# Loading the memory into a tile of x, turning it among the last sums, and reordering the loads and scalings around a pooling mixer

## The chip, the cores and the metric

The program runs on one core of a Trainium2 chip, in one launch. The metric is the device time of one execution in microseconds (us); lower is better. Before the change three runs took 1949.14, 1951.25 and 1950.2 us, so the median is 1950.2 us.

## What is computed

The reference is a decoder trunk over 512 tokens of width 1024, batch 1, depth 2. Each of the two layers is: half a SwiGLU feed-forward network (FFN), a token mixer, cross-attention into 256 memory tokens, a second half FFN. Each of the four ends in `X = LayerNorm(alpha * X + sublayer)`. Layer 0's mixer is a differential attention, layer 1's a causal pooling mixer. The two parts that the change touches are, cut to what matters:

```
def pool_mixer(x, w_grp, b_grp, scale):        # 4 groups of 256 columns, windows 2, 4, 8, 16
    pooled = (mean of the last w tokens) - x    # for each group g its own window w
    y = einsum('bsgc,gcd->bsgd', pooled, w_grp) + b_grp
    return y.reshape(B, S, D) * scale

def memory_cross_attention(x, mem, wq, wkv, wo):
    q = x @ wq                                  # 4 heads of 256
    k, v = split(mem @ wkv, 2)                  # 256 memory tokens
    o = softmax(q k^T / 16) v, head by head
    return o @ wo
```

All inputs are float32.

## The kernel before

**Numbers.** TensorE works in float32r, a rounded form of float32. Every operand is therefore split in two, `split` (L116): ScalarE (ACT) casts it to the high part (L119, names that end in `h`), VectorE (DVE) subtracts that from the source to get the low part (L120, names in `l`). A product is three matmuls, high by high, high by low, low by high (`mm3`, L198, shown as L202, L203, L204). A weight block of 1024 by 256 (1 MB) arrives as one `raw` tile and is split in two halves of 128x1024, that is two casts and two subtractions.

**X and its factors.** X lives as four token tiles of 128x1024. For matmuls it is split, where needed after a turn (a TensorE transpose), into factors that lie in the two `xh` and two `xl` tiles, which each phase claims anew (`new_xt`, L453).

**The place of the change** is layer 1, between the end of its first FFN and its cross-attention. The FFN's last products are sums into tokens, `plain_down` (L858), in the order of the table `LAST`, eight of them, each 18 matmuls of 128x512 (`ps<-ha,xe`, `ps<-hb,xe`). After a token's second sum its LayerNorm runs (`ln_token`, L361, with the long DVE operations at L379 and L381).

Then `mixer` (L1520) runs two things beside each other. `early_kv` (L1395) computes keys and values of the first two heads from the memory alone: `xa_kv` (L1323) loads the head's key weights (`raw_cols`, L230, `raw<-in_xa_wkv_dram`), makes 48 matmuls `pk`, loads the value weights, makes 48 matmuls `pv`, and does so for the second head. `pool_mixer` (L1237) makes the band products that pool over the windows (`pp`, eight chunks), splits each into `pooled`, multiplies by the pool's weights `pw`, adds to X (L357) and runs the LayerNorm token by token; after each LayerNorm the token is turned (L482) into factors for the cross-attention. `weave` (L207) interleaves the two on TensorE by a count of estimated time: a first step of the mixer after 4300 ns of key and value work, then one for every 900 ns. The cross-attention's queries (`xq`) follow.

Ahead of all this `load_memory` (L1297) loads `mem` into a tile of the `raw` pool and turns it, 16 transposes in four groups of four, each group into a PSUM bank of `aux`, and splits the result into `mem0h` to `mem6l`. `pool_weights` (L1202) loads the pool's weights (1 MB), and for each half of the columns a row of scales and a row of biases, each broadcast to 256 KB; it multiplies the weights by the scales (`pw<-pw,ps`, L1232) and prepares the bias.

**What sets the order.** All of these loads are issued by SyncE (SP) in one queue, in the order of the program, and SP waits at each load until its tile is free. `raw` has two buffers, so a load of weights waits until the splits of the load two before it are done. The rows of gain and bias for the LayerNorm (`load_row`, L325, issued at L334 as `pooled<-in_ln_g_dram` and `pooled<-in_ln_b_dram`) are in the same queue and take tiles of the tag `pooled`. Within an engine the instructions stand in an order that a scheduler fixes when the program is built, from priorities and dependencies; `issue_after` keeps an instruction behind a given one. Pools of SBUF follow each other in the order in which they are opened (`stage_pools`, L168), and a tile of a new pool waits until whatever of the old phase lay there is done.

Of the kernel before, what the change touches and what calls it, by code (L numbers as in the profile page):

```python
# [9 lines left out]
F32 = mybir.dt.float32  # L10
# [3 lines left out]
ALU = mybir.AluOpType  # L14
# [3 lines left out]
P = 128  # L18
D = 1024
S = 512  # L20
# [89 lines left out]
class Trunk:  # L110
# [56 lines left out]
    @contextmanager  # L167
    def stage_pools(self, w, raw, order):  # L168

        with ExitStack() as ctx:  # L170
            self.stage = {}
            for n in order:
                if n == "wl" and order[0] == "mem" or n == "wh" == order[0]:
                    self.to_w(ctx)
                self.stage[n] = ctx.enter_context(self.pool(n))
            self.banks = {n: ctx.enter_context(self.pool(n, space=PSUM)) for n in ("px", "py", "yz")}
            self.w_bufs, self.raw_bufs, self.aux_turn = w, raw, 0
            yield
# [679 lines left out]
    def plain_down(self, w, layer, j, ln, beside):  # L858
# [35 lines left out]
        for n, (half, t) in enumerate(LAST):  # L894
            if n == 2:
                if (layer, j) == (1, 0):
                    self.pool_bands()
                self.begin_ln(layer, ln, 2.0)
                for k in (1, 2):
                    operand(0, k)  # L900
                for tok in range(2):
                    for k in (1, 2):
                        product(sums[tok], 0, tok, k)
                    self.summed(0, tok, 1.0, sums[tok])
            ps = self.aux("ps", ("yz", "py")[n % 2])
            if n < 2:
                sums.append(ps)
                product(ps, half, t, 0)
                yield
                continue  # L910
            for k in range(3):
                if t == 0:
                    operand(half, k)
            if self.last_ln and t == NT - 1:
                parts = [(ps, slice(0, S))]
                if half:
                    parts = [(ps[:, : 2 * P], slice(0, 2 * P))]
# [281 lines left out]
            self.bandl, braw[:, :, 1, :16], self.bandf[:, :, :16].bitcast(F32)  # L1199
        )  # L1200

    def pool_weights(self):  # L1202

        nc = self.nc
        w = self.a["pool_w"][0].rearrange("g k n -> (g k) n")
        self.pool_w = self.tmp("pw", (P, KC, 256))
        nc.sync.dma_start(self.pool_w, w.rearrange("(k p) n -> p k n", p=P))
        rows = self.a["pool_b"].rearrange("l g c -> l (g c)")

        bias = self.pair("pb")  # L1210
        for half in range(2):
            c = slice(half * S, (half + 1) * S)
            sc, bs = self.tmp("ps"), self.tmp("ps")
            nc.sync.dma_start(sc, self.a["pool_scale"][:, c].to_broadcast([P, S]))
            nc.sync.dma_start(bs, rows[:, c].to_broadcast([P, S]))
            nc.vector.tensor_tensor(bs, bs, sc, ALU.mult)
            nc.vector.tensor_scalar(
                bias[half].rearrange("p (a n) -> p a n", n=P),
                self.ident[:, None].to_broadcast([P, NT, P]),
                0.0,  # L1220
                None,
                ALU.mult,
            )
            nc.scalar.copy(bias[half][:1], bs[:1])
            nc.scalar.copy(bias[half][32:33], bs[32:33])
            nc.vector.tensor_sub(
                bias[half][32:33], bs[32:33], bias[half][32:33].bitcast(F32)
            )
            for g in range(2):
                r = self.pool_w[:, 4 * half + 2 * g : 4 * half + 2 * g + 2]  # L1230
                f = sc[:, None, g * 256 : (g + 1) * 256].to_broadcast([P, 2, 256])
                nc.vector.tensor_tensor(r, r, f, ALU.mult)  # L1232
# [64 lines left out]
    def load_memory(self, tag=None):  # L1297
# [6 lines left out]
                for h in range(2):  # L1304
                    nc.sync.dma_start(raw[m][h], src[:, m, h])
        else:
            t = self.raw_tile((2, 2, S))
            nc.sync.dma_start(t, src)
            raw = [[t[:, m, h] for h in range(2)] for m in range(2)]
        self.memT = []  # L1310
        for c in range(0, KC, 2):
            pt = self.aux("pt").rearrange("p (c m n) -> p c m n", c=2, m=2)
            for i in range(2):
                for m in range(2):
                    o = (c + i) % 4 * P
                    self.nc.tensor.transpose(pt[:, i, m], raw[m][c // 4][:, o : o + P], self.ident)
            t = tuple(self.stage["mem"].tile([P, 2, MEM], F32R, name=f"mem{c}{n}") for n in "hl")
            self.split(t[0], t[1], pt.rearrange("p c m n -> p c (m n)"))
            self.memT += [(t[0][:, i], t[1][:, i]) for i in range(2)]
        if tag and LINE < 480:  # L1320
            self.stage["mem"].tile([P, (480 - LINE) // 4], F32, name="mempad")

    def xa_kv(self, w, h):  # L1323
        nc = self.nc
        rk = self.raw_cols(w, h * 256)
        ps = self.mm("pk").rearrange("p (c n) -> p c n", c=2)
        for j in range(2):
            wk = self.cols(rk, j)
# [7 lines left out]
        kt = kv()  # L1336
        self.turn_late()
        self.split(kt[0], kt[1], ps)
        wv = self.wide(self.raw_cols(w, D + h * 256))
        ps = self.mm("pv").rearrange("p (m n) -> p m n", m=2)  # L1340
        for m in range(2):
            o = slice(m * P, (m + 1) * P)
# [49 lines left out]
            self.oT.append(o)  # L1392
            yield

    def early_kv(self, layer, heads):  # L1395
        for h in range(heads):
            self.kv.append((yield from self.xa_kv(self.a["xa_wkv"][layer], h)))

    def xa_main(self, layer):
        wq, wkv = self.a["xa_wq"][layer], self.a["xa_wkv"][layer]  # L1400
# [119 lines left out]
    def mixer(self, layer, ln):  # L1520
# [65 lines left out]
```

## Time and profile before

| | before |
|---|---|
| median of three runs (lowest, highest) | 1950.2 us (1949.14, 1951.25) |
| span of the profiled execution | 1944.6 us |
| median less that span | 5.6 us |
| TensorE (PE) busy | 98% of the span |
| VectorE (DVE), ScalarE (ACT), GpSimd (POOL) busy | 81%, 53%, 15% |

The page shows one profiled execution; its own time is not listed apart from its span, and the median of the runs stands 5.6 us above the span. Views say which engine is busy (PE matmuls, PEld weight loads beside them), in which stretch, at which granted TensorE clock (PEclk, 1.00 is full speed), and what ended each wait ("idle before <- releaser"). Times of rows are us from the start of the span. A row's busy time of a matmul includes its way through the pipeline, so 171 matmuls of 278 ns fit in 20 us; their pitch, the number in a full stretch, is what one more costs.

### The profile page before, as it was taken

The page shows a single profiled execution, that of the slowest core. Times are in us where ns is not written, and L with a number is a line of the kernel's source. Part 1 is how long each engine was busy: PE and PEld are TensorE (multiplying, and loading weights), DVE is VectorE, ACT ScalarE, POOL GpSimd, SP SyncE. Part 2 cuts the span into 40 slices and gives each one's busy share as a digit, 9 for nine tenths or more (in the row PEclk, how much of TensorE's full clock was granted, in tenths as well). Part 3 has the DMA queues.
Part 4 walks back from the last instruction along what each step waited for, and adds up shares of the span by engine and source line. Part 5 has one row for each costly group of instructions (what it writes and reads, how often), then busy time and mean ns, then how long its engine had stood idle before and what let it go on. Part 6 is the DMA issues. An engine that isn't in the chain of part 4 may idle for free.

```text
span 1944.6 us, 32554 instructions
## 1 busy us (share of the span) xinstructions
PE 1913.0 (98%) x13122; PEld 1748.4 (90%) x13122; DVE 1566.7 (81%) x2215; ACT 1025.8 (53%) x1582; POOL 300.0 (15%) x266
## 2 busy tenths in 40 slices
PE   8999999999999999999999999999999999999998
PEld 8999998888778888999998999999888889999997
DVE  7888889888867557888888988898787458988886
ACT  6555554566655434655554655555455336555553
POOL 2112121111210001211220311212000003111210
PEclk9999999999999999999999999999989999999999
DMA  9978772322134316977785687877254338877861
GB/s 239 218 163 185 167 144 77 90 68 85 44 119 141 109 66 184 185 174 162 143 193 174 109 180 163 183 168 153 78 173 131 104 107 155 176 163 171 183 132 60
DMA packets 247031, 277.96 MB, mean 143 GB/s; under 512 B 8288, under 2 KB 212576, under 8 KB 246880
## 3 DMA queue, kind: packets, MB, share of 16 engines
q0 software_dynamic: 92928, 92.29, 31.1%
q1 hardware_dynamic: 153952, 183.59, 29.4%
q8 instruction: 103, 1.69, 0.4%
q14 instruction: 48, 0.39, 0.1%
HBM read 273.75 MB, written 2.10 MB: 142 GB/s over the span
## 4 chain that ended last, share of the span: by engine, by line
PE 82%; DVE 10%; issue 4%; ACT 2%; DMA 1%; POOL 1%; SPq 0%; DVEq 0%; POOLq 0%; ACTq 0%
PE x L202 7%; PE x L203 7%; PE x L204 7%; PE z L203 4%; PE z L202 4%; PE z L204 4%; PE ps L202 3%; PE ps L204 3%; PE ps L203 3%; PE px L202 2%; PE px L204 2%; PE px L203 2%; PE x L674 2%; DVE wl L120 2%; PE y L204 2%
## 5 line engine op out<-in xcount | busy, mean ns | idle before, releaser
L659 POOL DMA_DIRECT2D ra<-in_ffn_w_in_dram x132 | 170.2, 1303 | 1002.8 <-DVE wl L120 701.2
L119 ACT CAST wh<-ra 128x1024 fp32r<-128x1024 f32 x184 | 193.7, 1053 | 225.3 <-PE x L203 70.5
L120 DVE TENSOR_TENSOR wl<-ra,wh 128x1024 fp32r<-128x1024 f32 x184 | 224.6, 1224 | 72.0 <-ACT wh L119 71.2
L119 ACT CAST wh<-rc 128x1024 fp32r<-128x1024 f32 x136 | 143.2, 1053 | 121.6 <-PE x L203 41.9
L202 PE MATMUL x<-xe,wh 128*128 128x256 f32 x704 | 195.4, 278 | 0.0
L203 PE MATMUL x<-xe,wh 128*128 128x256 f32 x704 | 195.2, 277 | 0.0
L204 PE MATMUL x<-xe,wl 128*128 128x256 f32 x704 | 195.1, 277 | 0.0
L120 DVE TENSOR_TENSOR wl<-rc,wh 128x1024 fp32r<-128x1024 f32 x136 | 165.1, 1223 | 29.1 <-ACT wh L119 28.8
L119 ACT CAST wh<-b 128x1024 fp32r<-128x1024 f32 x112 | 117.8, 1052 | 134.2 <-PE x L203 68.7
L120 DVE TENSOR_TENSOR wl<-b,wh 128x1024 fp32r<-128x1024 f32 x112 | 137.1, 1224 | 41.3 <-ACT wh L119 41.3
L202 PE MATMUL x<-xh,wh 128*128 128x256 f32 x544 | 151.3, 278 | 0.0
L203 PE MATMUL x<-xl,wh 128*128 128x256 f32 x544 | 150.9, 277 | 0.0
L204 PE MATMUL x<-xh,wl 128*128 128x256 f32 x544 | 150.9, 277 | 0.0
L203 PEld LDWEIGHTS x<-xe,wh 128*128 128x128 f32 x704 | 132.5, 188 | 1.3
L202 PEld LDWEIGHTS x<-xe,wh 128*128 128x128 f32 x704 | 132.1, 188 | 1.3
L204 PEld LDWEIGHTS x<-xe,wl 128*128 128x128 f32 x704 | 132.5, 188 | 0.0
L120 DVE TENSOR_TENSOR wl<-raw,wh 128x1024 fp32r<-128x1024 f32 x64 | 80.6, 1265 | 54.5 <-ACT wh L119 53.8
L203 PEld LDWEIGHTS x<-xl,wh 128*128 128x128 f32 x544 | 102.5, 188 | 0.7
L202 PEld LDWEIGHTS x<-xh,wh 128*128 128x128 f32 x544 | 102.1, 188 | 0.7
L119 ACT CAST wh<-raw 128x1024 fp32r<-128x1024 f32 x64 | 66.7, 1050 | 68.1 <-PE xq L203 22.6
L204 PEld LDWEIGHTS x<-xh,wl 128*128 128x128 f32 x544 | 102.4, 188 | 0.0
L204 PE MATMUL y<-xh,wl 128*128 128x256 f32 x352 | 98.4, 280 | 1.0 <-DVE wl L120 0.2
(436 smaller groups left out, 6331.4 us busy)
## 6 DMA issues: line engine op xcount, KB each, us to landing
ra<-in_ffn_w_in_dram POOLq DMA_DIRECT2D x132, 512.0 KB, 6.8
rc<-in_ffn_w_in_dram SPq DMA_DIRECT2D x88, 512.0 KB, 5.8
b<-in_ffn_w_out_dram SPq DMA_DIRECT2D x76, 512.0 KB, 4.7
ra<-in_ffn_w_in_dram SPq DMA_DIRECT2D x44, 512.0 KB, 5.3
rc<-in_ffn_w_in_dram POOLq DMA_DIRECT2D x44, 512.0 KB, 7.0
raw<-in_xa_wkv_dram SPq DMA_DIRECT2D x16, 1024.0 KB, 5.5
raw<-in_da_w_qkv_dram SPq DMA_DIRECT2D x16, 512.0 KB, 5.1
raw<-in_xa_wq_dram SPq DMA_DIRECT2D x8, 1024.0 KB, 5.1
```

The lines of the kernel that those rows point to most:

```text
L119: self.nc.scalar.copy(hi, src),
L120: self.nc.vector.tensor_sub(lo, src, hi.bitcast(F32)),
L202: mm(out, w[0], x[0], start=start, stop=False, skip_group_check=again)
L203: mm(out, w[0], x[1], start=False, stop=False, skip_group_check=again)
L204: self.last_mm = mm(out, w[1], x[0], start=False, stop=stop, skip_group_check=again)
L659: nc.gpsimd.dma_start(t, source(*block), accum_op=ALU.add)
L674: self.last_mm = nc.tensor.matmul(ps[:, j], v[i][:, k, j * P : (j + 1) * P], x[l][:, k], start=n == i == l == 0, stop=n == 7 and i == 1, s ...
```

## The change

Five things are changed, all of them in layer 1 between the FFN and the cross-attention.

1. The memory is loaded into a tile of `xtp` with the tag `xh` (named `memraw`), not into a tile of `raw`. All its 16 turns are placed behind one matmul, `amid`, the last of the third of the eight sums of `plain_down` (n == 2 there); their four PSUM tiles come from `mm`, `px` and `aux`.
2. The key and the value weights of head 0 are both requested ahead of the mixer and handed to `xa_kv` as `raws`.
3. `pool_weights` is cut in two. `pool_loads` requests the weights and all four rows at once (`ps` has four buffers now), `pool_weights` does the scaling, and is called after the pooled chunk 1, behind that chunk's split on DVE. The zeros and ones that DVE wrote (three `tensor_scalar`) are three memsets on POOL.
4. The pools are opened in the order `wh`, `wl`, `mem`, `raw`, with the pads of `to_w` and `to_x` ahead of `wh` and `mem`.
5. The numbers of `weave` are 640 and 8500 for 900 and 4300.

```diff
-                if n == "wl" and order[0] == "mem" or n == "wh" == order[0]:
+                if n == "wh" == order[0]:
                     self.to_w(ctx)
+                if n == "mem":
+                    self.to_x(ctx)
...
             self.summed(half, t, 1.0, ps)
+            if n == 2:
+                self.amid = self.last_mm
             few(beside, 6)
...
-    def pool_weights(self):
+    def pool_loads(self):
...
         nc.sync.dma_start(self.pool_w, w.rearrange("(k p) n -> p k n", p=P))
-        rows = self.a["pool_b"].rearrange("l g c -> l (g c)")
-
-        bias = self.pair("pb")
+        self.ones, self.pool_b = self.act("ones", (P, P)), self.pair("pb")
+        rows, self.pool_rows = self.a["pool_b"].rearrange("l g c -> l (g c)"), []
         for half in range(2):
...
             nc.sync.dma_start(bs, rows[:, c].to_broadcast([P, S]))
+            self.pool_rows.append((sc, bs))
+
+    def pool_weights(self):
+
+        nc, bias = self.nc, self.pool_b
+        nc.gpsimd.memset(self.ones.bitcast(F32), 1.0)
+        for half, (sc, bs) in enumerate(self.pool_rows):
+            nc.gpsimd.memset(bias[half].bitcast(F32), 0.0)
             nc.vector.tensor_tensor(bs, bs, sc, ALU.mult)
-            nc.vector.tensor_scalar(
...
-            )
...
-        self.ones = self.act("ones", (P, P))
-        nc.vector.tensor_scalar(self.ones, self.ident, 0.0, 1.0, ALU.mult, ALU.add)
-        self.pool_b = bias
...
         yield
-        self.pool_weights()
         for c in range(KC):
+            if c == 2:
+                with self.tc.issue_after(split[1].ins):
+                    self.pool_weights()
...
-            self.split(q[0], q[1], pp)
+            split = self.split(q[0], q[1], pp)
...
-            t = self.raw_tile((2, 2, S))
+            t = self.xtp.tile([P, 2, 2, S], F32, tag="xh", name="memraw")
             nc.sync.dma_start(t, src)
...
+            pt = self.aux("pt") if tag else self.aux("pt", "px") if c % 4 else self.mm("pt")
...
+            with nullcontext() if tag else self.tc.issue_after(self.amid.ins):
...
-    def xa_kv(self, w, h):
+    def xa_kv(self, w, h, raws=None):
         nc = self.nc
-        rk = self.raw_cols(w, h * 256)
+        rk = raws[0] if raws else self.raw_cols(w, h * 256)
...
-        wv = self.wide(self.raw_cols(w, D + h * 256))
+        wv = self.wide(raws[1] if raws else self.raw_cols(w, D + h * 256))
...
-            self.later.enter_context(self.other_pools(("mem", "wl", "raw", "wh")))
+            self.later.enter_context(self.other_pools(("wh", "wl", "mem", "raw")))
+            self.to_w(self.later)
             self.kvp = self.later.enter_context(self.pool("kv"))
-            bufs = dict(pw=1, pb=2, ps=2, ones=1, _x=0, pooled=20, sq=1)
+            bufs = dict(pw=1, pb=2, ps=4, ones=1, _x=0, pooled=20, sq=1)
...
+                w = self.a["xa_wkv"][layer]
+                raws = [self.raw_cols(w, c) for c in (0, D)]
+                self.pool_loads()
                 next(side)
                 self.kv = []
-                self.weave(self.early_kv(layer, 2), side, 900, 4300)
+                self.weave(self.early_kv(layer, 2, raws), side, 640, 8500)
```

Lines of the changed kernel are two to nine higher than those of before (L202 is L204, L230 is L232, L334 is L336, L357 is L359, L379 and L381 are L381 and L383).

**SP's queue.** Before, from the memory's load to the rows of the mixer's LayerNorm; the four loads `raw<-in_xa_wkv_dram` are key and value weights of head 0 and of head 1:

```order
L1308 DMA raw<-in_mem_dram 128x2x1024
L1193 DMA hb<-in_band_dram 128x1152
L230 DMA raw<-in_xa_wkv_dram 128x8x256
L1207 DMA pw<-in_pool_w_dram 128x8x256
L230 DMA raw<-in_xa_wkv_dram 128x8x256
L1214 DMA ps<-in_pool_scale_dram 128x512
L1215 DMA ps<-in_pool_b_dram 128x512
L230 DMA raw<-in_xa_wkv_dram 128x8x256 x2
L1214 DMA ps<-in_pool_scale_dram 128x512
L1215 DMA ps<-in_pool_b_dram 128x512
L230 DMA raw<-in_xa_wq_dram 128x8x256
L334 DMA pooled<-in_ln_g_dram 128x512 x2
```

Now the same stretch, from the table of bands on (the memory's load, L1311, stands further up, ahead of the gain row of the FFN's LayerNorm); the first pair `raw<-in_xa_wkv_dram` is head 0, the second head 1, the single one head 2's keys:

```order
L1197 DMA hb<-in_band_dram 128x1152
L232 DMA raw<-in_xa_wkv_dram 128x8x256 x2
L1217 DMA ps<-in_pool_scale_dram 128x512
L1218 DMA ps<-in_pool_b_dram 128x512
L1211 DMA pw<-in_pool_w_dram 128x8x256
L1217 DMA ps<-in_pool_scale_dram 128x512
L1218 DMA ps<-in_pool_b_dram 128x512
L232 DMA raw<-in_xa_wkv_dram 128x8x256 x2
L232 DMA raw<-in_xa_wq_dram 128x8x256
L232 DMA raw<-in_xa_wkv_dram 128x8x256
L336 DMA pooled<-in_ln_g_dram 128x512 x2
L336 DMA pooled<-in_ln_b_dram 128x512 x2
```

Head 0's two weight blocks stand together, all five of the pool's loads stand ahead of head 1's weights, and the LayerNorm rows stand behind head 2's key weights, not ahead of them.

**DVE.** Before, from the value weights of head 0 on; `wl<-raw` are weight splits, `pw<-pw,ps` scalings of the pool's weights:

```order
L120 TENSOR_TENSOR wl<-raw,wh 128x1024
L120 TENSOR_TENSOR kv<-pk,kv 128x512
L120 TENSOR_TENSOR wl<-raw,wh 128x1024
L1216 TENSOR_TENSOR ps<-ps 128x512
L1232 TENSOR_TENSOR pw<-pw,ps 128x512
L120 TENSOR_TENSOR wl<-raw,wh 128x1024
L1226 TENSOR_TENSOR pb<-ps,pb 1x512
L120 TENSOR_TENSOR pooled<-pp,pooled 128x512
L120 TENSOR_TENSOR wl<-pw,wh 128x1024
L120 TENSOR_TENSOR pooled<-pp,pooled 128x512
L1232 TENSOR_TENSOR pw<-pw,ps 128x512 x2
```

Now, from the key weights of head 1 (first row) to the second split of head 1's value weights (the last `wl<-raw` of the second piece), in two pieces that follow each other:

```order
L120 TENSOR_TENSOR wl<-raw,wh 128x1024 x2
L120 TENSOR_TENSOR pooled<-pp,pooled 128x512 x2
L120 TENSOR_TENSOR kv<-pv,kv 128x512
L1227 TENSOR_TENSOR ps<-ps 128x512
L1236 TENSOR_TENSOR pw<-pw,ps 128x512 x2
L1227 TENSOR_TENSOR ps<-ps 128x512
L1230 TENSOR_TENSOR pb<-ps,pb 1x512
L1236 TENSOR_TENSOR pw<-pw,ps 128x512 x2
```

```order
L120 TENSOR_TENSOR pooled<-pp,pooled 128x512
L1230 TENSOR_TENSOR pb<-ps,pb 1x512
L120 TENSOR_TENSOR pooled<-pp,pooled 128x512
L120 TENSOR_TENSOR wl<-pw,wh 128x1024
L120 TENSOR_TENSOR pooled<-pp,pooled 128x512
L120 TENSOR_TENSOR wl<-pw,wh 128x1024
L120 TENSOR_TENSOR wl<-raw,wh 128x1024
L120 TENSOR_TENSOR pooled<-pp,pooled 128x512
L120 TENSOR_TENSOR wl<-raw,wh 128x1024
```

All scaling of the pool's weights stands behind the splits of head 1's key weights and of the first two pooled chunks; before, the first scaling stood among head 0's splits.

**PE.** Before, at the end of the FFN's last sum; half of the memory's turns stand between the first products of `pk`:

```order
L204 MATMUL ps<-ha,xe 128x512
L202 MATMUL pk<-mem0h,wh 128x256
L203 MATMUL pk<-mem0l,wh 128x256
L204 MATMUL pk<-mem0h,wl 128x256
L1316 MATMUL pt<-ident,raw 128x128 x4
L202 MATMUL pk<-mem0h,wh 128x256
L203 MATMUL pk<-mem0l,wh 128x256
L1316 MATMUL pt<-ident,raw 128x128 x4
```

Now all sixteen stand between two of the sums:

```order
L205 MATMUL ps<-ha,xe 128x512
L206 MATMUL ps<-ha,xe 128x512
L1321 MATMUL pt<-ident,memraw 128x128 x16
L204 MATMUL ps<-hb,xe 128x512
L205 MATMUL ps<-hb,xe 128x512
```

And between the end of the last sum and the first band product there stand 48 matmuls of `pk` and 39 of `pv`; before there were 48 of `pk`, 8 turns and 3 of `pv`.

More of the change, by code (lines that the diff above doesn't have):

```diff
@@ L1215, in pool_weights @@
             nc.sync.dma_start(bs, rows[:, c].to_broadcast([P, S]))
-            nc.vector.tensor_tensor(bs, bs, sc, ALU.mult)
[L1217 to L1222, printed above, removed]
-            )
+            self.pool_rows.append((sc, bs))
[4 more added lines that the diff above has]
+            nc.gpsimd.memset(bias[half].bitcast(F32), 0.0)
+            nc.vector.tensor_tensor(bs, bs, sc, ALU.mult)
             nc.scalar.copy(bias[half][:1], bs[:1])
@@ L1311, in load_memory @@
         for c in range(0, KC, 2):
[L1312 to L1316, printed above, removed]
+            pt = self.aux("pt") if tag else self.aux("pt", "px") if c % 4 else self.mm("pt")
+            pt = pt.rearrange("p (c m n) -> p c m n", c=2, m=2)
+            with nullcontext() if tag else self.tc.issue_after(self.amid.ins):
+                for i in range(2):
+                    for m in range(2):
+                        o = (c + i) % 4 * P
+                        self.nc.tensor.transpose(
+                            pt[:, i, m], raw[m][c // 4][:, o : o + P], self.ident
+                        )
             t = tuple(self.stage["mem"].tile([P, 2, MEM], F32R, name=f"mem{c}{n}") for n in "hl")
@@ L1393, in xa_head, with early_kv @@
             yield
-    def early_kv(self, layer, heads):
+    def early_kv(self, layer, heads, raws):
         for h in range(heads):
-            self.kv.append((yield from self.xa_kv(self.a["xa_wkv"][layer], h)))
+            self.kv.append((yield from self.xa_kv(self.a["xa_wkv"][layer], h, raws)))
+            raws = None
     def xa_main(self, layer):
```

## Prediction

> **What bounds the kernel now.** I read the page first: span, busy shares and the chain of work that ended last.
>
> ```profile
> span 1944.6 us, 32554 instructions
> PE 1913.0 (98%) x13122; PEld 1748.4 (90%) x13122; DVE 1566.7 (81%) x2215; ACT 1025.8 (53%) x1582; POOL 300.0 (15%) x266
> PE 82%; DVE 10%; issue 4%; ACT 2%; DMA 1%; POOL 1%; SPq 0%; DVEq 0%; POOLq 0%; ACTq 0%
> ```
>
> TensorE is busy for 98% and carries 82% of the chain. The change takes no matmul away, so it can gain only where PE waits or runs slowly, and lose only where it makes PE wait. Next I read the windows over the stretch that the diff touches: the last sums, the hand-over to the key products, the first value and pool products, the rest of the mixer.
>
> ```profile
> core 0: us, PE busy (x) PEld busy (x) DVE busy (x) ACT busy (x) POOL busy (x), PEclk, DMA share, GB/s
> 1393.00:1413.00 20.00, 20.00 (x91) 16.46 (x90) 16.09 (x27) 8.34 (x17) 3.67 (x3) 1.00 0.00 1
> 1413.00:1423.50 10.50, 7.24 (x55) 6.25 (x52) 9.49 (x17) 5.57 (x11) 1.41 (x1) 1.00 0.92 302
> 1423.50:1434.00 10.50, 9.49 (x45) 9.49 (x46) 8.23 (x10) 5.25 (x7) 0.00 (x0) 0.51 0.62 197
> 1434.00:1454.00 20.00, 20.00 (x171) 19.81 (x171) 15.48 (x24) 10.49 (x16) 0.88 (x1) 1.00 0.51 157
> 1454.00:1479.00 25.00, 23.50 (x190) 22.11 (x188) 22.67 (x41) 14.23 (x24) 2.01 (x3) 1.00 0.20 65
> ```
>
> In 1393 to 1413 PE never rests and the DMA engines stand still (share 0.00). In the 10.5 us after that PE is busy for 7.24 while DMA runs at 0.92. In the next 10.5 us the granted clock is 0.51. From 1434 on PE is full again, and from 1454 DVE is nearly full too (22.67 of 25). The view of PE's waits from 1380 to 1480 names what it waited for:
>
> ```profile
> PE pv L202 <- ACT wh L119: 1.7, 1, 1.7
> PE pv L203 <- DVE wl L120: 1.2, 1, 1.2
> PE pt L482 <- DVE X L381: 1.0, 1, 1.0
> PE pk L202 <- ACT mem2h L119: 0.6, 1, 0.6
> PE pk L204 <- DVE wl L120: 0.5, 1, 0.5
> ...
> PE pk L203 <- DVE mem2l L120: 0.3, 1, 0.3
> ```
>
> The five of `pk` and `pv` are the hand-over: 1.7 + 1.2 + 0.6 + 0.5 + 0.3 = 4.3 us. The longest is head 0's value weights. ScalarE cast them at
>
> ```profile
> 1421.87 1.04 ACT L119 CAST wh<-raw 128x1024 fp32r<-128x1024 f32 x1 [1.09 <-DMA raw<-in_xa_wkv_dram]
> ```
>
> as soon as they landed, having waited 1.09 us for the transfer.
>
> **The change part by part. (a) Head 0's weights early, memory out of `raw`.** SP's own rows show why the value weights were late:
>
> ```profile
> 1380.93 0.37 SPq L230 DMA_DIRECT2D raw<-in_xa_wkv_dram  x1
> 1412.69 0.37 SPq L1207 DMA_DIRECT2D pw<-in_pool_w_dram  x1
> 1414.16 0.37 SPq L230 DMA_DIRECT2D raw<-in_xa_wkv_dram  x1
> ...
> 1441.22 1.05 SPq L334 DMA_DIRECT2D pooled<-in_ln_g_dram  x2
> 1442.31 1.10 SPq L334 DMA_DIRECT2D pooled<-in_ln_b_dram  x2
> ```
>
> Keys went out at 1380.93; values stood behind the pool weights, whose tile came free at 1412.69 with the last sums, and went out at 1414.16. Now both stand ahead of it, and the memory no longer holds one of the two `raw` buffers, so values go out with the keys, in the stretch where DMA idles. The four splits are then done among the last sums, and the five waits of 4.3 us fall.
>
> The half clock falls with them, I take it. Its price: 45 products took 9.49 us; at the pitch of the next row (20.00 us for 171, 0.117 us) they take 5.3, so it cost 4.2. Together PE reaches the mixer's products 4.3 + 4.2 = **8.5 us** earlier. What is left of waiting there: 87 key and value products (48 and 39) stand ahead of the first band product, 87 x 0.117 = 10.2 us, so PE asks for the last token's factor at 1412.5 + 10.2 = 1422.7. DVE made it in
>
> ```profile
> 1420.32 1.29 DVE L120 TENSOR_TENSOR xl<-X,xh 128x512 fp32r<-128x512 f32 x2
> ```
>
> ready at 1421.6; two more weight splits and a key split stand ahead of it now, and the memory's four splits and the zeros do not: earlier or later by about a microsecond, cost 0 to 0.6, and hidden in any case behind what follows in (c).
>
> [...]
>
> **(b) The 16 turns, the zeros and ones.** The turns cost PE what they did:
>
> ```profile
> 1385.57 1.03 PE L1316 MATMUL pt<-ident,raw 128*128 128x128 f32 x8
> ...
> 1412.85 0.60 PE L1316 MATMUL pt<-ident,raw 128*128 128x128 f32 x4
> ```
>
> Eight take 1.03 us wherever they stand, so 16 take 2.1 before and after. Their place, behind the third sum, is past the memory's landing: its load moves up ahead of the bands. If the memory were late PE would stand still there with the remaining sums behind the turns; the DMA share of 0.00 from 1393 speaks against a jam. Cost 0; the worst is one transfer, the 7.5 us of the transfers' view below, and I take none of it. The zeros and ones leave DVE:
>
> ```profile
> L1217 DVE TENSOR_SCALAR pb<-ident 128x512 fp32r<-128x512 f32 x2 | 0.8, 423 | 0.0
> ```
>
> 0.8 us less on DVE ahead of the last token's factor, which is counted above. On POOL, which is idle in most of this stretch (0.00 busy in the window from 1423.5), three memsets come in their place, and by this kernel's other memsets, 64x512,
>
> ```profile
> L1181 POOL MEMSET low<- 64x512 f32 x4 | 2.1, 521 | 34.4 <-DVE wl L120 34.2
> ```
>
> they take 0.5 us each, 1.6 in all. They can delay the bias alone, which is wanted 15 us later: 0.
>
> **(c) The pool's loads at once, the scaling later: what is late next.** The five pool loads (4 x 256 KB and 1024 KB) and head 1's key weights (1024 KB) now stand in one row, 3072 KB, all behind the tile that comes free at about 1412.5. Transfers there:
>
> ```profile
> raw<-in_xa_wkv_dram SPq DMA_DIRECT2D x4, 1024.0 KB, 7.5
> pw<-in_pool_w_dram SPq DMA_DIRECT2D x1, 1024.0 KB, 5.5
> ps<-in_pool_scale_dram SPq DMA_DIRECT2D x2, 256.0 KB, 7.4
> ...
> pooled<-in_ln_g_dram SPq DMA_DIRECT2D x2, 256.0 KB, 7.0
> pooled<-in_ln_b_dram SPq DMA_DIRECT2D x2, 256.0 KB, 7.4
> ```
>
> Before, the first three of the row (pool weights, values, scales, 2304 KB) had landed when DVE's wait ended:
>
> ```profile
> 1422.63 0.69 DVE L1232 TENSOR_TENSOR pw<-pw,ps 128x512 f32<-128x512 f32 x1 [1.01 <-DMA ps<-in_pool_scale_dram]
> ```
>
> 2304 KB in 1422.63 - 1412.69 = 9.9 us, so 3072 KB take 13.3 and land at 1425.8. By the 302 GB/s of the window they take 10.4 and land at 1422.9. I take the middle, 1424.4. Behind them stand, on DVE, 17 rows of the new order: 6 weight splits and 15 operations of 512 wide, from head 1's keys to its last value split. The starts of neighbours give their pitches:
>
> ```profile
> 1441.88 0.68 DVE L120 TENSOR_TENSOR kv<-pv,kv 128x512 fp32r<-128x512 f32 x1
> 1442.48 1.22 DVE L120 TENSOR_TENSOR wl<-raw,wh 128x1024 fp32r<-128x1024 f32 x1
> 1443.61 0.69 DVE L120 TENSOR_TENSOR pooled<-pp,pooled 128x512 fp32r<-128x512 f32 x1
> ```
>
> 0.60 for a 512-wide operation and 1.13 for a weight split. So 6 x 1.13 + 15 x 0.60 = 15.8 us. With the cast ahead of the first (1.04, the row above) and 0.7 for small waits on casts, DVE frees the `raw` tile of head 1's values at 1424.4 + 1.0 + 15.8 + 0.7 = 1441.9. **SP waits for just that**: head 2's keys want this tile, and the LayerNorm's rows, for which the whole mixer ends, now stand behind that load instead of ahead of it. They go out at 1442.3 to 1443.9 (0.4 for the load ahead, 1.05 and 1.10 for the rows), against 1441.22 to 1443.41 before. By their medians the last bias row lands at 1443.9 + 7.4 = 1451.3, less some tenths since both halves go by one median; the second half of the first token's norm (0.67, half of its 1.41 for two) ends at about 1452.1. Before it ended at the start of the next operation:
>
> ```profile
> 1453.14 1.41 DVE L381 SCALAR_TENSOR_TENSOR X<-X,rstd,pooled 128x512 f32<-128x512 f32 x2
> 1454.47 0.68 DVE L357 SCALAR_TENSOR_TENSOR X<-X,ps 128x512 f32<-128x512 f32 x1
> ...
> 1455.68 0.69 DVE L120 TENSOR_TENSOR kv<-pk,kv 128x512 fp32r<-128x512 f32 x1
> ```
>
> 1454.47 against 1452.1: of the 8.5 us only **2.4** are left at the first token. The split of head 1's keys, 0.60, stood between token 0 and token 1 and stands ahead of token 0 now, in the time that DVE waits for the rows anyway. From there to the last queries' first product,
>
> ```profile
> 1478.64 0.50 PE L202 MATMUL xq<-xh,wh 128*128 128x256 f32 x2 [0.47 <-ACT xh L119]
> ```
>
> the order of DVE and PE is that of before (PE full, DVE 22.67 of 25), so 2.4 + 0.6 = 3.0 us arrive there, and behind it nothing that differs stands in the order. The other 5.5 us PE waits: for pooled splits around 1440 and for the first token around 1450.
>
> **(d) Pools and `weave`.** They take no instruction away; what they do to the order is counted above (87 products, the DVE rows). The second FFN's first loads swap places; PE was never seen to wait for such loads in the stretch shown, so 0, at best -0.5.
>
> **Sum.** -8.5 + 5.5 = -3.0 us: span 1944.6 - 3.0 = 1941.6. The profiled span stands 5.6 us under the median of the runs, 1950.2, and I carry that over: **1947.2 us**.
>
> **The rivals.** *R1, the half clock comes back elsewhere.* The 5.5 us that PE now waits lie in two places, of some 2 to 3 us each. Before, 1.7 + 1.2 us of waiting within 2 us brought the half clock, while the single 1.0 us for X at 1469 did not. So a wait of 2 to 3 us may bring it. Price: 0 to 4.2, and as PE then runs against DVE for part of it, some 2.9: 1950.1, no change. [...]
>
> *R2, slower: head 1's keys land late.* Six transfers share one queue; at the 197 GB/s of the window from 1423.5 the 3072 KB take 16.0 us and land at 1428.5. Then the LayerNorm rows land 4.1 us later than I took, the first token ends at 1456.2, and PE, which waits the whole of it in one piece, gets the half clock as well: -3.0 + 4.1 + 4.2 gives 1955.5. It decides from a landing of about 1427.4 (3.0 later than taken, 211 GB/s). For it speaks that a broadcast row of 256 KB took 7.4 us from issue where 1024 KB took 5.5; against it, the 9.9 us for 2304 KB with one such row inside.
>
> *R3, more is kept.* At 302 GB/s keys land 1.5 us earlier, and if the rows land in 6 us rather than 7.4 another 1.4 is won: 1944.3. If the rows were not late at all, all of 8.5 would stay: 1941.7. For it speaks that only the two `raw` loads run beside the rows then.
>
> That the change doesn't do what it says could be if values waited for another tile all the same; then (a) gives nothing and (c) still moves the rows: this lies in R2's range.
>
> **How the numbers follow.** The forecast, 1945.7 to 1948.5, gets 0.42; R1, 1948.5 to 1951, 0.27; R3, 1941.7 to 1945.7, 0.18; R2, 1951 to 1957, 0.13. The range from 1943.5 to 1951.5 leaves out about a quarter of R3 and most of R2, 0.15 together. A measurement of this kernel can tell about 0.2% from no change, 3.9 us: under 1946.3 is faster, over 1954.1 slower. Faster: R3 and two fifths of the forecast, 0.35. Slower: three quarters of R2, 0.10. The rest, 0.55, is the same.
>
> **What would show it.** No waits of `pk` and `pv` and a PEclk of 1.00 from 1413 to 1434 show (a) right. PE's waits must then name `pooled` near 1440 and X before the first turn L484, of 2 us or more each; and DVE's norm (L381) must wait for a DMA of `pooled<-in_ln_g` or `in_ln_b`. Head 1's keys should be cast first at 1424 to 1426. If the norm waits for no DMA, (c) is wrong and the gain is larger; if PEclk is under 1 between 1440 and 1460, R1 came; if the cast is at 1427 or later, R2.

## The result, and the profile after

In twenty executions each the changed kernel took 1943.13 us (median; 1938.9 to 1948.7) and the kernel of before 1947.7 (1943.56 to 1957.37): a ratio of 0.9975, interval 0.9966 to 0.9984, so 4.9 us less by the ratio (3.1 to 6.6); the two medians differ by 4.6. The forecast was 3.0 us less, 1947.2 us, with a range from 1943.5: the time lies 0.4 us under the range. Beside the experiments the changed kernel was timed again: 1941.47 (11 executions) against 1947.74 (27), ratio 0.9968 (0.9957 to 0.9980).

The executions of the changed kernel above, and all of both kernels in the later measurements, are listed with their span and their mean granted TensorE clock, and these two columns carry the study. (The twenty of before above have only their times.) A half clock of 10 us would take 0.0026 from the mean clock, by arithmetic (half of 10 over a span of 1944.6). Time less span is 1.72 to 1.84 us in the 20 of the changed kernel above and in the 88 of before in the later measurements. By mean clock they fall into three classes:

| mean clock | before: executions, mean span | after: executions, mean span |
|---|---|---|
| 0.995 and under | 36, 1948.6 us | 4, 1945.4 us |
| 0.996 and 0.997 | 38, 1945.1 us | 16, 1940.9 us |
| 0.998 and over | 14, 1940.6 us | 11, 1939.8 us |

The column after has the 20 executions above and the 11 of the second timing. Where the clock was full the two kernels differ by 0.8 us, no more than the scatter of such small groups; in the middle class they differ by 4.2 us and in the lowest by 3.2. So the changed kernel gains mostly in executions that have half clocks, in two ways. It has fewer: its mean clock is 0.9968 over all, that of before 0.9959. And those it has cost less. By the lowest and the highest class of before, 0.001 of mean clock goes with 1.7 us, so the 0.0009 would give about 1.6 us by my estimate, of a difference in mean span of 4.7 us (1945.8 to 1941.1).

The profiled execution of the changed kernel has a mean clock of 0.994, as only 4 of its 31 executions have or less; that of before has 0.997. Its windows, with the columns and stretches of those of before:

```profile
1393.00:1413.00 20.00, 20.00 (x93) 16.55 (x92) 16.04 (x25) 10.05 (x19) 5.19 (x6) 1.00 0.06 17
1413.00:1423.50 10.50, 10.50 (x92) 10.50 (x91) 8.27 (x11) 3.91 (x7) 1.35 (x1) 1.00 1.02 330
1423.50:1434.00 10.50, 9.25 (x55) 8.84 (x53) 7.97 (x12) 6.56 (x10) 0.00 (x0) 0.71 0.45 152
1434.00:1454.00 20.00, 20.00 (x114) 19.81 (x114) 12.25 (x19) 8.80 (x14) 0.03 (x1) 0.64 0.34 106
1454.00:1479.00 25.00, 23.37 (x189) 21.75 (x188) 23.65 (x43) 13.33 (x23) 2.66 (x4) 1.00 0.19 64
```

From 1413 to 1423.5 PE is full (10.50, before 7.24): the hand-over is mended. But PEclk falls to 0.71 and 0.64 in the next two, and 114 products take the 20 us in which 171 were done. Ahead of that PE waited twice for head 1's key weights:

```profile
PE pk L206 <- DVE wl L120: 0.8, 1, 0.8
PE pk L204 <- ACT wh L119: 0.5, 1, 0.5
```

The same kernel in an execution with 0.998 (label e1):

```profile
1413.00:1423.50 10.50, 10.50 (x87) 10.34 (x86) 9.73 (x14) 5.79 (x9) 2.03 (x3) 1.00 0.88 291
1423.50:1434.00 10.50, 10.50 (x92) 10.34 (x92) 8.05 (x12) 6.24 (x9) 0.00 (x0) 1.00 0.65 210
1434.00:1454.00 20.00, 16.34 (x126) 15.14 (x126) 16.19 (x29) 9.91 (x17) 0.54 (x1) 0.99 0.34 106
1454.00:1479.00 25.00, 23.58 (x179) 22.14 (x178) 22.08 (x37) 12.56 (x21) 1.82 (x3) 0.94 0.28 92
```

Here PE rests from 1434 to 1454 (16.34 of 20), as forecast. The 0.99 and the 0.94 are one half clock of 3.5 us from 1453.6 on, behind the wait for X. PE's longest waits from 1413 to 1480:

```profile
PE pt L484 <- DVE X L383: 1.9, 1, 1.9
PE ps L206 <- DVE pooled L120: 1.7, 2, 1.1
PE xq L204 <- DVE kv L120: 0.6, 1, 0.6
```

No `pk` and no `pv` is among its waits; the pooled splits and X have taken their place. And DVE's norm of the first token waits for the rows of gain that SP sent late:

```profile
1443.11 0.37 SPq L232 DMA_DIRECT2D raw<-in_xa_wkv_dram  x1
1443.53 1.05 SPq L336 DMA_DIRECT2D pooled<-in_ln_g_dram  x2
```

```profile
1449.78 1.41 DVE L381 SCALAR_TENSOR_TENSOR X<-X,mean,pooled 128x512 f32<-128x512 f32 x2 [3.35 <-DMA pooled<-in_ln_g_dram]
1451.15 1.41 DVE L383 SCALAR_TENSOR_TENSOR X<-X,rstd,pooled 128x512 f32<-128x512 f32 x2
1452.49 0.68 DVE L359 SCALAR_TENSOR_TENSOR X<-X,ps 128x512 f32<-128x512 f32 x1
```

**A measure for the experiments.** Executions start their layers some us apart (the first key product stood at 1410.0 to 1414.4 in the profiles), so I compare a length: *the stretch*, from the first key product to the first product of the last queries. In before it runs from 1412.49 to 1478.64, 66.15 us:

```profile
1412.49 0.28 PE L202 MATMUL pk<-mem0h,wh 128*128 128x256 f32 x1
```

In e1 it is 61.69, in the profile after 66.82:

```profile
1413.91 0.28 PE L204 MATMUL pk<-mem0h,wh 128*128 128x256 f32 x1
```

```profile
1475.60 0.50 PE L204 MATMUL xq<-xh,wh 128*128 128x256 f32 x2 [0.47 <-ACT xh L119]
```

```profile
1412.03 0.28 PE L204 MATMUL pk<-mem0h,wh 128*128 128x256 f32 x1
```

```profile
1478.85 0.38 PE L204 MATMUL xq<-xh,wh 128*128 128x256 f32 x1 [0.56 <-ACT xh L119]
```

Behind the stretch the profiles agree with before within 1 us (but for e8 and e12, see there); the changed kernel takes 0.4 us less there. Ahead of it, from the row of gain that SP requests in layer 1's first FFN to the first key product, it takes 0.7 us longer than before, as eight turns moved there.

### The profile page after: what moved, and what is told of

Same layout as the page of the kernel before. It is cut to its first block, busy times and chain, and to the rows that moved or that the text cites. A ratio compares the mean times of both kernels' runs of the same rounds, so it can differ in the third digit from the quotient of the medians.

```text
span 1944.4 us, 32555 instructions
## 1 busy us (share of the span) xinstructions
PE 1916.4 (99%) x13122; PEld 1753.2 (90%) x13122; DVE 1565.4 (81%) x2212; ACT 1025.2 (53%) x1582; POOL 300.3 (15%) x269
## 4 chain that ended last, share of the span: by engine, by line
PE 80%; DVE 10%; issue 4%; ACT 3%; DMA 2%; POOL 1%; SPq 1%; DVEq 0%; POOLq 0%; ACTq 0%
PE x L204 7%; PE x L205 7%; PE x L206 7%; PE z L205 4%; PE z L204 4%; PE z L206 4%; PE ps L204 3%; PE ps L206 3%; PE ps L205 3%; PE px L204 2%; PE px L206 2%; PE px L205 2%; DVE wl L120 2%; PE y L206 2%; PE x L676 2%
## 5 line engine op out<-in xcount | busy, mean ns | idle before, releaser
L204 PE MATMUL x<-xe,wh 128*128 128x256 f32 x704 | 195.5, 278 | 0.0
L204 PE MATMUL x<-xh,wh 128*128 128x256 f32 x544 | 151.4, 278 | 0.0
L204 PEld LDWEIGHTS x<-xe,wh 128*128 128x128 f32 x704 | 132.3, 188 | 1.3
L204 PEld LDWEIGHTS x<-xh,wh 128*128 128x128 f32 x544 | 102.2, 188 | 0.7
```

What stands on the lines that cost most here:

```text
L204: mm(out, w[0], x[0], start=start, stop=False, skip_group_check=again)
```

## The experiments

Theory A: the gain hangs on the half clock. Theory B, part (c) of the prediction: it hangs on what ends the mixer, the rows of the LayerNorm and DVE. All ratios are to before on the same chip; the measurements are spread over four chips, so medians of different labels are not to be compared closely.

| label | ratio, interval | executions, median us | mean clock | of these at 0.995 or less | profile: clock, stretch |
|---|---|---|---|---|---|
| e1_after_again | 0.9968, 0.9957 to 0.9980 | 11, 1941.47 | 0.9967 | 2 | 0.998, 61.7 |
| e2_weave_old | 0.9972, 0.9956 to 0.9988 | 12, 1940.69 | 0.9969 | 1 | 0.997, 60.1 |
| e3_scale_early | 0.9979, 0.9959 to 0.9998 | 11, 1944.64 | 0.9950 | 7 | 0.994, 66.4 |
| e4_after_fill | 0.9969, 0.9953 to 0.9986 | 9, 1940.51 | 0.9980 | 0 | 0.998, 60.8 |
| e5_keys_first | 0.9958, 0.9943 to 0.9973 | 7, 1938.48 | 0.9981 | 0 | 0.999, 59.7 |
| e6_rows_early | 0.9951, 0.9926 to 0.9975 | 7, 1939.30 | 0.9980 | 0 | 0.998, 58.1 |
| e7_keys_rows | 0.9955, 0.9935 to 0.9974 | 8, 1937.54 | 0.9980 | 0 | 0.998, 56.5 |
| e8_before_fill | 0.9970, 0.9956 to 0.9983 | 11, 1942.64 | 0.9985 | 0 | 0.999, 62.1 |
| e9_pool_old | 0.9973, 0.9951 to 0.9995 | 8, 1942.31 | 0.9959 | 3 | 0.995, 64.4 |
| e10_mem_only | 0.9981, 0.9969 to 0.9992 | 11, 1943.37 | 0.9973 | 0 | 0.997, 61.5 |
| e11_scale_early_fill | 0.9951, 0.9934 to 0.9968 | 5, 1937.99 | 0.9986 | 0 | 0.999, 57.9 |
| e12_before_half_fill | 0.9988, 0.9972 to 1.0004 | 12, 1945.96 | 0.9967 | 4 | 0.998, 61.9 |

**e1_after_again**, the changed kernel unaltered.

> The changed kernel once more, unaltered, as the measure for the others. Its profile was of an execution with a mean clock of 0.994, one of the two lowest of twenty, and showed a half clock from 1428.0 to 1448.5. Theory A (the gain hangs on the half clock): an execution with a mean clock of 0.998 shows no half clock between 1413 and 1480 and a span 3 to 5 us under that of one with 0.994. Theory B (the end of the mixer hangs on the rows of the LayerNorm and on DVE): the span is the same within 1 us whatever the clock. Time against before 0.9975 by both.

The stretch is 5.1 us and the span 3.2 us shorter at 0.998 than at 0.994. That is what A expected, though a half clock of 3.5 us did come; B's 1 us did not, as far as one profile of each can tell. B's mechanism is there too: it is what sets the 61.7. The half clock after head 1's keys lasted 20.5 us (shown at the end), which alone would cost 10.2 by its clock of 0.50. About 3.7 us of that fell where PE rests anyway at a full clock (16.34 of 20), and e1 has 1.7 of its own, which leaves 4.8 by this estimate for the 5.1 measured. So only 5.1 of the 10.2 us show between the two profiles, as by this estimate a part of this half clock fell into a rest of PE.

**e8_before_fill**, the test of the clock by itself:

```diff
+        if h == 0 and self.ln_next == "pool":
+            pt = self.aux("pt", "px")
+            with self.behind():
+                for i in range(22):
+                    j = i % 4 * P
+                    nc.tensor.transpose(pt[:, j : j + P], self.ident, self.ident)
         wv = self.wide(self.raw_cols(w, D + h * 256))
```

> The kernel of before with 22 idle turns of the identity (2.9 us) ahead of the first value product, where PE waited 1.7 and 1.2 us. It computes the same, and all its loads and splits stay. Theory A: PE does not pause, the half clock from 1423 to 1434 does not come, the mean clock rises by 0.001 or more, and the time falls by 2 to 4 us: 0.998 to 0.999 of before; that part of the change's gain then comes from the clock and not from the 4.3 us of waits. [...]

```profile
1413.00:1423.50 10.50, 8.49 (x67) 1.00 1.01 331
1423.50:1434.00 10.50, 10.50 (x94) 1.00 0.51 161
1434.00:1454.00 20.00, 20.00 (x168) 1.00 0.47 159
```

These windows (PE busy, PEclk, DMA share, GB/s) show a full clock where before had 0.51. The value weights came no earlier, 22 turns of pure waste were added, and the stretch fell from 66.15 to 62.1, 4.1 us; the ratio, 0.9970, is like that of the changed kernel. So the half clock of the hand-over follows from PE's waits there, and keeping it away is worth as much as the whole change. It isn't shown that the change gains by the clock alone: e8 has a mean clock of 0.9985, the changed kernel 0.9967 and the same ratio. Open: what lies behind the stretch took 1.9 us longer in this profile (3.2 in that of e12) than before, which no part of the edit explains.

**e12_before_half_fill**, the same with 11 turns.

> The kernel of before with 11 idle turns (1.45 us) ahead of the first value product where 22 (2.9 us) kept the clock full. About half of the 2.9 us of waiting is left. If the half clock follows from the sum of PE's pauses within a few us, it should come in fewer executions than before (mean clock 0.997 to 0.998, time 0.998 of before). If any pause brings it, as 1.3 us did among the band products in the changed kernel, the mean clock stays at 0.996 and the time at 0.9995 to 1.000. If only a pause of 1.7 us in one piece brings it, the clock is as full as with 22 turns, 0.9985, and the time 0.997.

The mean clock is 0.9967 (before on the same chip 0.9954). Six of 12 executions are at 0.998 or over, against 14 of 88 of before and 10 of 11 with 22 turns; four are at 0.995 or less, a share like that of before (36 of 88). The spans are 1941.7 us in the six and 1948.6 in the four. Its profiled execution has waits of 0.5 and 1.1 us left at that place and a mean clock of 0.998. The first reading, that the half clock comes by the amount of pausing in a few us, fits the mean clock best, but 12 executions do not settle it, and the interval reaches to no change.

**e4_after_fill**, 12 such turns in the changed kernel, ahead of head 1's first key product (in `early_kv`, `if h:`).

> The changed kernel with 12 idle turns of the identity on PE (1.6 us) ahead of head 1's first key product, where PE waited 0.5 and 0.8 us for the weights and the half clock followed. It computes the same. Theory A: PE has no pause there, the clock stays at 1.00 from 1413 to 1450, the mean clock is 0.998 in nearly all executions, and the time is 1 to 2 us less than that of the changed kernel although 0.5 to 1 us of work were added: 0.997. Theory B: added work on PE is hidden or costs, 0.9975 to 0.998, and the clock does not matter.

The mean clock is 0.998, with no execution under 0.996 (4 of 31 of the changed kernel were at 0.995 or less). The gain in time, 0.8 us of span by the means against e1, is too small to tell. Between e4 and e8, both kernels with the clock kept up, no difference is seen: 0.9969 and 0.9970.

**e5_keys_first**, head 1's keys ahead of the pool's weights:

```diff
...
                 raws = [self.raw_cols(w, c) for c in (0, D)]
+                raws[0] = [self.cols(raws[0], j) for j in range(2)]
+                self.next_keys = self.raw_cols(w, 256)
                 self.pool_loads()
...
```

> The changed kernel with head 1's key weights requested ahead of the pool weights and of the second rows of scale and bias (they were behind all five). They land 4 to 5 us earlier, about 1420, so PE's two waits of 0.5 and 0.8 us for them go. DVE splits them ahead of the last token's factor. Theory A: no half clock there, mean clock 0.998, time 0.9965 of before, 2 us less than the changed kernel. Theory B: the splits only move, DVE has the same work ahead of the LayerNorm's rows; SP issues them 1 to 3 us earlier, as DVE no longer starts its row at 1425.9; 0.996 to 0.997, with the clock playing no part. If the last token's factor is now late (two splits of 1.13 ahead of it), PE waits there and the time is that of the changed kernel.

Both held: the mean clock is 0.998 and the stretch 2.0 us under that of e1. By ratio it is ahead of the changed kernel (0.9958 to 0.9968), but the intervals overlap.

**e6_rows_early** and **e7_keys_rows** request the mixer's rows of gain and bias ahead of head 2's keys, in the changed kernel and in e5:

```diff
...
+            if c == 4:
+                self.wide_gain = False
+                gb = [self.load_row("pooled", self.a[n][layer, ln]) for n in ("ln_g", "ln_b")]
...
-        self.begin_ln(layer, ln, 1.0)
+        self.begin_ln(layer, ln, 1.0, gb)
```

> The changed kernel with the mixer's rows of gain and bias requested before head 2's key weights (they stood behind). In an execution of the changed kernel with a full clock DVE's first norm waited 3.35 us for them. Theory B (the end of the mixer hangs on these rows): that wait goes, the first turn of X comes about 38.1 - 3.4 = 34.8 us after the first key product, and the time falls by up to 3.4 us: 0.9955 of before. Rival: PE has the products to fill the 3.4 us no better later, DVE was only early, and something else is late next (the sums of the pool's output, or the last token's norm, which ends a row of DVE work that is nearly full): under 1 us, 0.997.

> Both edits: head 1's keys ahead of the pool weights, and the rows of gain and bias ahead of head 2's keys. If each wait is a link of the same chain, the two gains add: keys first gave 1.9 us in the stretch from the first key product to the last queries (61.7 to 59.8) and the rows would give up to 3.4 more: 0.994 of before. If one hides the other, it is that of keys first alone, 0.996.

The stretch falls by 3.6 us (61.7 to 58.1) and by 3.2 (59.7 to 56.5): in the stretch the gains add. In time that isn't seen: e7's ratio, 0.9955, is not under e6's 0.9951 and did not reach the 0.994 of its expectation. DVE's waits between 1440 and 1460 in e6 hold no DMA any more:

```profile
DVE X L381 <- ACT sq L377: 0.6, 1, 0.6
DVE X L359 <- PE ps L206: 0.2, 1, 0.2
```

At a full clock theory B is right, and its link is this load of rows. e7 has the shortest stretch and the lowest median, 1937.54 us, but e6, e7 and e11 can't be told apart by their ratios (0.9951, 0.9955, 0.9951). In e7 PE is full in the window where it rested in e1:

```profile
1434.00:1454.00 20.00, 19.92 (x160) 1.00 0.22 73
```

**e2_weave_old**, `weave` at 900 and 4300.

> The changed kernel with the old numbers of weave (900 and 4300). The band products then stand behind 51 products and not 87, so PE asks for the last token's factor at about 1418.5, while DVE has it at about 1422: a wait of 3 us. Theory A: that wait brings the half clock in every execution, mean clock 0.997 or less, and 3 to 5 us of the gain are lost: 0.999 to 1.000 of before. Theory B: the wait is covered, since the end of the mixer hangs on DVE and the rows: 0.9975 within 0.0005.

Each theory had half of it right: A the mean clock (0.9969), B the ratio (0.9972 lies in its 0.9975 within 0.0005), though not for B's reason. PE waits 1.8 us for the last token's factor (3 were expected) and the clock is halved for some 3.4 us (by my estimate from the windows: 0.99 from 1413 and 0.85 from 1423.5, of 10.5 us each), but the loads fall back in place with the old numbers: the rows go out ahead of head 2's keys.

```profile
1437.93 1.04 SPq L336 DMA_DIRECT2D pooled<-in_ln_g_dram  x2
1439.02 0.92 SPq L336 DMA_DIRECT2D pooled<-in_ln_b_dram  x2
1443.00 0.38 SPq L232 DMA_DIRECT2D raw<-in_xa_wkv_dram  x1
```

What the wait costs the rows give back. The new numbers themselves therefore put the rows behind that load.

**e3_scale_early** and **e11_scale_early_fill**, the scaling at `c == 0`, without and with 20 idle turns ahead of head 1's keys.

> The changed kernel with the scaling of the pool's weights at its old place, ahead of the first pooled chunk; the loads stay early. DVE has 8 operations of 0.6 us more ahead of the first two pooled splits and the same number less behind them. Theory B: the row of DVE up to the release of head 1's last value weights is as long, so nothing changes: 0.9975 within 0.0007. Rival: the scaling waits for the pool weights' landing (about 1422) with the splits of head 1's keys behind it, PE waits 2 to 4 us more there, and the half clock comes in most executions: 0.9985 to 1.000.

> The changed kernel with the scaling at its old place (7 of 11 executions at a mean clock of 0.994 or less, the others 1935 to 1938 us of span) and 20 idle turns (2.6 us) ahead of head 1's first key product. Theory A: late scaling is worth nothing but the clock; with the turns the clock stays full in nearly all executions and the median span is 1936 to 1939, 0.9955 of before, less than the changed kernel with its turns (1938.7 to 1939.9). Rival: scaling early costs DVE time by itself, and the fast executions of it were chance: 0.997 or more with a clock of 0.998.

In e3's profile there is one wait of 1.20 us for head 1's keys, and then:

```profile
1426.00:1429.50 3.50, 2.30 (x19) 1.00 0.12 39
1429.50:1450.00 20.50, 20.50 (x98) 0.50 0.47 154
```

Seven of 11 executions were at 0.994 or less and took 1944.5 to 1948.1 us; the four others took 1934.5 to 1940.8 us. So the ratio of e3, 0.9979, which is B's number, is a mean of two kinds; the clock is what the rival named. With the turns all five are at 0.998 or over and the ratio is 0.9951, so those four were not chance. Late scaling thus is no gain to DVE. It even costs, by one profile of each: SP could request head 2's keys, with the rows behind them, 26.0 us after the first key product in e11's profile and 29.2 us in e1's, since late scaling stands on DVE between head 1's key and value splits. What it is worth is that the clock stays up more often (4 of 31 executions at 0.995 or less, 7 of 11 in e3). That PE waits less for head 1's keys is not shown: 1.2 us in e3, 1.3 in the profile after, none in e1.

**e9_pool_old**, the scaling at its old place and `weave` undone, and **e10_mem_only**, the memory's part alone in the kernel of before.

> The changed kernel with the pool's part undone: the loads are recorded beside the scaling again, the scaling ahead of the first pooled chunk, weave 900 and 4300; the memory in a tile of x, both weights of head 0 early and the order of the pools stay. The rows of gain and bias stand ahead of head 2's keys again. By now: at a full clock the stretch from the first key product to the last queries is some 58 us (the changed kernel 61.7 with its 3.4 us wait for the rows, 58.1 without), but DVE scales ahead of head 1's splits, so PE waits 1 us or more for these and for the last token's factor, and the half clock comes in half of the executions or more: mean clock 0.995 to 0.996, 0.997 to 0.998 of before. Rival: the early weights of head 0 alone remove the half clock: mean clock 0.998, 0.995.

> The kernel of before with the memory's part alone: the memory in a tile of x, its 16 turns behind the third sum. As a raw tile is then free, head 0's value weights go out ahead of the pool's weights even without the edit that asks for them. If the hand-over waits of before (4.3 us and the half clock behind them) hang on that tile, they go: mean clock 0.998 and 0.997 or less of before, the same as before with idle turns. Rival: the value weights' splits now stand in DVE's way ahead of the last token's norm and the waits only change their place: 0.999 to 1.000.

In e9 SP's queue kept the new order of the pool's loads, so they are not undone, though the edit records them later; the memsets stay on POOL too. The run has the clock that was expected (0.9959); in its profile PE waits 2.2 us for the last token's factor with a PEclk of 0.50 behind it.

In e10 the value weights did go out early, but one wait of 3.5 us for the low part of head 0's key weights, which DVE makes behind the last but one token's factors, took the place of the five: the waits changed their place, as the rival had it. The half clock that follows lasts 3.3 us only (windows of PE busy, PEclk, DMA share, GB/s):

```profile
PE pk L204 <- DVE wl L120: 3.5, 1, 3.5
```

```profile
1412.00:1416.00 4.00, 0.46 (x4) 0.98 0.71 233
1416.00:1419.30 3.30, 3.30 (x17) 0.50 0.58 208
1419.30:1423.00 3.70, 3.70 (x33) 1.00 0.85 271
```

No execution of e10 was under 0.996. The memory's part alone has a ratio of 0.9981, between the two expectations and most of the way to 0.9975 and 0.9968, with one wait longer than any of the five of before and a shorter half clock behind it.

## Why the prediction was wrong, and where it was right

- **The base is what failed**: "The profiled span stands 5.6 us under the median of the runs, 1950.2, and I carry that over". What lies around the span is 1.7 to 1.8 us, so the profiled execution of before took about 1946.4 us; the other 3.8 us are the difference between that execution and the middle one of three others. Twenty executions of before have their median at 1947.7, 2.5 us under that of the three: of the 4.1 us by which the forecast was too high, 2.5 are the base. That the three had less luck with the clock would fit, but their clocks are not listed. Three runs from 1949.14 to 1951.25 looked like a narrow spread and were not one.
- The other 1.6 us are the gain, 4.6 by the medians where 3.0 were forecast. The forecast span, 1941.6, with 1.8 is 1943.4, and 1943.13 was measured; that this is so close is in part luck, since the profiled execution of before was 1.3 us faster than the median of the twenty.
- (a) The five waits went: right. The half clock's price, 4.2 us: right, e8 measured 4.1. That it "falls with them": right in most executions only. The term was mis-sized as a single event of one profile: of before 36 of 88 executions were at 0.995 or less, with 8.0 us more span by the mean than the 14 at 0.998 and over, and 4 of 31 of the changed kernel. How the average gain divides between fewer half clocks and cheaper ones is an estimate above and not shown by a run.
- (b) 0, and 0.7 us of turns merely moved: right.
- (c) Head 1's keys were to land at 1424.4; the cast began at 1424.90. The rows were to go out at 1442.3; in e1, which stands 1.4 us later in all, at 1443.53. The first norm was to end at 1452.1, in e1's time 1453.5, and ended at 1452.49: the bias rows landed in 6.4 us by the median in e1, where the forecast took 7.4. The wait of PE at the pooled splits and at X: seen, 1.7 and 1.9 us, where 5.5 in all and 2 or more each were forecast.
- (d) was counted at 0, and the numbers of `weave` are what moved the rows (e2). The effect was in the sum, under the wrong name.
- What (c) gives back is what keeps the change from showing a gain at a full clock: its stretch (61.7, and 0.7 more ahead of it) is that of before with idle turns (62.1).
- The sum of -3.0 us for an execution of before with 0.997 and one after with 0.998: spans 1944.6 and 1941.2, -3.4.
- R1 came in two forms. In e1 the half clock stood at the place that was named, behind the wait for X, but for 3.5 us only, and after waits as long (1.6 us in e4, 2.2 in e5) it did not come. In the profile after, it stood at a place that I had not named (0.5 and 0.8 us of waiting for head 1's keys) and cost 5.1 us against e1 rather than 2.9. R2 did not come. The measured time lies in the range of R3, and the rows did land sooner, but most of what took it there is the base; most of R3's gain is what e6 and e7 took.

## What to carry to other kernels

Where PE is nearly full, read a pause first by what the clock does after it: filling it with idle work is a cheap test of what the half clock behind it costs (here 4.1 us). Compare executions by their mean clock before explaining a difference of 0.2%, and take the time around the span from runs that list both. When loads share one queue, look at which load each one now stands behind: small rows behind a big load that waited for its tile made DVE wait 3.4 us here.

## What the runs showed of the hardware

Single waits of 0.5 to 3.5 us stood ahead of the half clocks in the profiles. In before they were 1.7 and 1.2 us with a PEclk of 0.51 behind them; in e8, where idle turns filled most of these (0.7 was left), it was 1.00. In the profile after PE was busy for 1.75 of 3 us before it, in e3 for 2.30 of 3.5, with single waits of 0.5, 0.8 and 1.2 us. The profile after, then e1 around its wait for X:

```profile
1425.00:1428.00 3.00, 1.75 (x12) 1.00 0.15 47
1428.00:1448.50 20.50, 20.50 (x97) 0.50 0.38 117
```

```profile
1450.20:1453.60 3.40, 1.51 (x11) 1.00 0.19 74
1453.60:1457.10 3.50, 3.50 (x19) 0.51 0.00 0
```

In the first the half clock held 20.5 us although PE had no pause in them (20.50 busy); in e1 3.5 us at 0.51 followed a stretch with 1.51 busy of 3.40. In e5 a single wait of 2.2 us for X passed without any (PEclk 1.00 from 1434 to 1454 and on to 1479). The longest single wait, 3.5 us in e10, had 3.3 us at 0.50 behind it. How much waiting brings a half clock, whether that alone decides, and why some half clocks lasted 3.3 to 3.5 us and others 20.5, was not settled.
